# Loading the second block's x in steps between the columns of the first input projection

## The chip, the cores and the metric

The program runs on one core of one Trainium2 chip. The core has five engines that run their own queues of instructions: TensorE (PE: matmuls and transposes, which write PSUM; PEld is its loading of the fixed operand), VectorE (DVE), ScalarE (ACT), GpSimd (POOL, without access to PSUM) and SyncE (SP, which here asks for every DMA transfer). PSUM has eight banks of 512 float32 columns for 128 partitions. The metric is the device time of one execution in microseconds.

## The reference, cut to what matters

Two layers of a decoder trunk over 1040 tokens (16 meta tokens and 1024 of x) of width 1024. Each layer mixes the tokens and then applies an MLP:

```
h = concat(meta, x)
for layer in range(2):
    proj = rmsnorm(h) @ w_in[layer]          # 3336 columns, cut into the inputs of three mixers
    mixed = concat(hgrn2(...), gated_deltanet(...), s5(...))
    h = h + mixed @ w_out[layer]
    h = h + relu(rmsnorm(h) @ w1[layer])**2 @ w2[layer]
return rmsnorm(h)[:, 16:]
```

The gated DeltaNet's q, k and v (12 groups of 128 columns) pass through a causal convolution over four tokens and a SiLU; its gate z has four groups more. All is float32.

## The kernel before, in words

The 1040 tokens are two blocks of T = 520. Channels lie on partitions: a block's h is eight tiles of 128 x 520, of which there are eight buffers in all. Products are computed in three passes (high parts, low part of x, low part of w), 48 matmuls for a group of 128 columns ("a column" below), into a PSUM tile "pd" of two banks. There are two such tiles; every projection, the norm's scale and the loading of x take one in turn. Results pass through six SBUF tiles "s" of 128 x 520 on their way to DRAM.

`run` goes through block 0 and block 1 of the first layer, then the MLP of block 0, block 0 of the second layer (the third block of the program), and so on. `block` computes the norm, S5's two columns, the decay's rows, and then for each pair of heads four columns of q and k (`in_conv`, columns 0 to 7) and, window by window, the matrices of the DeltaNet (`gdn_decay`, which reads q and k back from DRAM). `gdn_solve` inverts their diagonal parts on VectorE and GpSimd, `s5_layer` prepares S5. Then come the columns 8 to 11 (v, again `in_conv`), four gates z (`in_gate`), and HGRN2's columns with its recurrence.

`early`, the generator that `block(0, 0)` gets as its `hook`, loads the second block's x. It takes the eight buffers of h after block 0's norm, calls `load_x(1, ...)` and then stores the second block's h to DRAM (`save_h`, eight transfers). `load_x` has ten parts, five windows of 104 tokens by two halves of 512 channels: a transfer into an "s" tile, four transposes on TensorE into one bank of a "pd" tile, four copies from there to h, by turns on ScalarE and VectorE. The block calls it whole, between `s5_layer` and column 8.

The order in the source is not the order of the queues: at build, a planner goes through the instructions with an estimate of their times and puts on each engine what is ready, the earlier in the source the sooner. The buffers of one name are given out in the order of the source. Two engines don't use one PSUM bank at the same time; the planner sets a wait between them. Weights are loaded ahead (`high_priority`).

Of the kernel before, what the change touches and what calls it, by code (L numbers as in the profile page):

```python
# [19 lines left out]
NMETA = 16  # L20
DEPTH = 2
T = 520
W = 104
# [7 lines left out]
NW = T // W  # L31
# [41 lines left out]
def pipeline(steps, gap):  # L73

    waiting, live, n = list(steps), [], 0
    while waiting or live:
        if waiting and n % gap == 0:
            live.append(waiting.pop(0))
        n += 1
        for g in list(live):  # L80
            if next(g, StopIteration) is StopIteration:
                live.remove(g)
        yield


def trace(*gens):

    live = list(gens)
    while live:
        for g in list(live):  # L90
            if next(g, StopIteration) is StopIteration:
                live.remove(g)


class Kern:
# [619 lines left out]
    def block(self, l, b, h, hook=None, first=False):  # L715

        xs = self.normed_rows(h, 8 * l, b)
        if first:
            self.save_h(b, h)
        self.Y = self.YS[b] = self.tl(self.dr, [KD, 128, T], "ydr", 2)  # L720
        if first:
            self.setup_mixers()
        g = {"z": self.tl(self.dr, [6, 128, T], "gated", 2)}
        us = self.in_s5(l, xs)
        g["rows"] = self.in_rows(l, b, xs)
        g["qkv"] = self.QKV = self.tl(self.dr, [12, 128, T], "qkvd", 2)
        self.gdn_begin(l, b, g)
        for p in range(2):
            for i in (2 * p, 2 * p + 1, 4 + 2 * p, 5 + 2 * p):
                self.in_conv(l, b, xs, i)  # L730
            trace(pipeline([self.gdn_decay(g, w, p) for w in range(NW)], GAP_DECAY))
        self.gdn_solve()
        self.gdn_scales()
        if b == 0:
            self.s5_layer(l)
        if hook:
            trace(hook)
        for i in range(8, 12):
            self.in_conv(l, b, xs, i)
        for i in range(4):  # L740
            self.in_gate(l, xs, C_GZ + 128 * i, g["z"][i])
        for j in range(2):
            hd = self.in_hgrn(l, xs, j)
            self.in_gate(l, xs, C_HG + 128 * j, g["z"][4 + j])
            trace(self.hgrn(l, b, j, hd, g["z"][4 + j]))
        self.grp = "t"
        trace(pipeline([self.gdn_state(l, g, w, p) for w in range(NW) for p in range(2)], GAP_STATE),
              self.lead(self.s5(l, b, us), AHEAD_S5))
        self.grp = "h"
# [499 lines left out]
    def load_x(self, b, h):  # L1249
        nc = self.nc  # L1250
        x = self.ins["x"][0]
        for w in range(NW):
            t0 = b * T + w * W - NMETA
            for k0 in (0, 4):
                xt = self.s()[:W, :512]
                cs = slice(128 * k0, 128 * k0 + 512)
                if t0 < 0:
                    nc.sync.dma_start(xt[0:NMETA, :], self.ins["meta"][:, cs])
                    nc.sync.dma_start(xt[NMETA:W, :], x[0:W - NMETA, cs])
                else:  # L1260
                    nc.sync.dma_start(xt, x[t0:t0 + W, cs])
                ps = self.tl(self.pd, [128, 2, 512], "pd", 2)[:, 0, :]
                for i in range(4):
                    nc.tensor.transpose(ps[:, i * W:(i + 1) * W], xt[:, i * 128:(i + 1) * 128], self.ident[:W, :W])
                for i in range(4):
                    copy = nc.vector.tensor_copy if i % 2 else nc.scalar.copy
                    copy(h[k0 + i][:, w * W:(w + 1) * W], ps[:, i * W:(i + 1) * W])
            yield

    def save_h(self, b, h):  # L1270
        self.H[b] = [self.spill(h[k], "hdr", 16) for k in range(KD)]
# [212 lines left out]
```

## Time and the profile before

| | us |
|---|---|
| median of three runs | 3055.49 |
| lowest and highest of the three | 3043.4 and 3062.02 |
| the profiled execution's own time | 3057.18 |
| its span, first to last instruction | 3055.4 |
| mean granted clock of TensorE in it, as a share of 2.4 GHz | 0.964 |

The profile is of one execution. Its times in rows are us from the first instruction; durations are us, or ns where that is said. A line such as L125 is the line of the kernel; helpers have one line for all their callers (L125 is every matmul, L113 every two-operand elementwise operation, L110 every activation), so the tiles' names tell them apart. In the views of waits, "A <- B" says that A stood still until B ended.

### The profile page before, as it was taken

What the parts mean: (1) busy time and instruction counts of PE and PEld (TensorE: products, weight loads), DVE (VectorE), ACT (ScalarE), POOL (GpSimd) and SP (SyncE); (2) the same over time, 40 slices, a digit from 0 to 9 for tenths busy, and PEclk for the clock granted to TensorE, in tenths of its full rate; (3) what the DMA queues carried; (4) which work ended last, traced back from release to release, by engine and by line L of the source; (5) the groups of instructions that cost most, each with busy time, mean ns of one, the idle gap of its engine ahead of it and who ended that gap; (6) DMA issues with size and microseconds to landing.
All of it is one profiled execution on the core that took longest, in us unless ns stands there. A gap on an engine that the chain in (4) does not pass through costs nothing.

```text
span 3055.4 us, 60525 instructions
## 1 busy us (share of the span) xinstructions
PE 2826.1 (92%) x23513; PEld 2637.9 (86%) x23513; DVE 1562.6 (51%) x2905; ACT 1298.7 (43%) x2657; POOL 1580.1 (52%) x1425
## 2 busy tenths in 40 slices
PE   7776899979999989878999998988999999999998
PEld 6775889978999989878999998986777788999998
DVE  7588664685532245787453224686554222522224
ACT  4434455534433345444444334543544333433332
POOL 4555465664644445747354444676464444444442
PEclk8898899989999999999999999999999999999999
DMA  5755555744433345555443334565443333533332
GB/s 148 193 125 160 141 154 138 213 95 125 126 96 96 91 141 142 161 142 149 130 115 96 94 91 142 144 152 152 113 125 98 100 96 95 163 91 90 93 91 80
DMA packets 641610, 381.17 MB, mean 125 GB/s; under 512 B 166239, under 2 KB 599237, under 8 KB 641325
## 3 DMA queue, kind: packets, MB, share of 16 engines
q1 hardware_dynamic: 641325, 377.31, 45.2%
q8 instruction: 186, 3.05, 0.4%
q14 instruction: 99, 0.81, 0.1%
HBM read 308.52 MB, written 70.43 MB: 124 GB/s over the span
## 4 chain that ended last, share of the span: by engine, by line
PE 45%; DVE 5%; issue 1%; DMA 1%; POOL 1%; ACT 1%; SPq 0%; DVEq 0%; POOLq 0%; ACTq 0%
PE pd L125 39%; PE mxt L125 4%; PE mxh L125 1%; DVE mh L113 1%; DVE s L116 1%; POOL wl L113 0%; DVE s L113 0%; ACT s L110 0%; DMA wr<-in_w_in_dram 0%; DVE s L121 0%; DMA nh<-rowd 0%; DVE mt L113 0%; POOL mh L113 0%; DVE ul L113 0%; DVE s L642 0%
## 5 line engine op out<-in xcount | busy, mean ns | idle before, releaser
L113 POOL TENSOR_TENSOR wl<-wr,wh 128x512 fp32r<-128x512 f32 x776 | 1025.2, 1323 | 1079.5 <-ACT wh L459 1012.3
L125 PE MATMUL pd<-xh,wh 128*128 128x260 f32 (+4 forms) x3688 | 832.3, 299 | 59.2 <-DVE s L116 21.2
L125 PE MATMUL pd<-xl,wh 128*128 128x260 f32 (+3 forms) x3688 | 830.1, 298 | 17.8 <-DVE xl L113 10.4
L459 ACT CAST wh<-wr 128x512 fp32r<-128x512 f32 x776 | 477.5, 617 | 862.5 <-PE pd L125 774.5
L125 PE MATMUL pd<-xh,wl 128*128 128x260 f32 (+2 forms) x3624 | 814.1, 299 | 11.0 <-POOL wl L113 10.7
L125 PEld LDWEIGHTS pd<-xh,wh 128*128 128x128 f32 (+1 forms) x3688 | 593.1, 192 | 81.4 <-issue 28.6
L125 PEld LDWEIGHTS pd<-xl,wh 128*128 128x128 f32 (+1 forms) x3688 | 594.4, 192 | 34.4 <-DVE xl L113 12.3
L125 PEld LDWEIGHTS pd<-xh,wl 128*128 128x128 f32 x3624 | 586.3, 193 | 27.2 <-POOL wl L113 13.5
L125 PE MATMUL pd<-uh,wh 128*128 128x260 f32 (+1 forms) x2008 | 469.5, 302 | 6.2 <-DVE h L113 3.6
L125 PE MATMUL pd<-ul,wh 128*128 128x260 f32 (+1 forms) x2008 | 470.5, 302 | 0.0
L125 PE MATMUL pd<-uh,wl 128*128 128x260 f32 (+1 forms) x2008 | 468.5, 302 | 1.2 <-POOL wl L113 1.2
L113 DVE TENSOR_TENSOR h<-h,pd 128x520 f32<-128x520 f32 (+2 forms) x296 | 200.4, 678 | 398.1 <-PE pd L125 395.5
L110 ACT ACTIVATE s<-s 128x520 f32<-128x520 f32 (+3 forms) x431 | 272.9, 635 | 196.5 <-DVE s L121 144.8
L125 PEld LDWEIGHTS pd<-uh,wh 128*128 128x128 f32 x2008 | 321.2, 189 | 22.3 <-issue 5.9
L125 PEld LDWEIGHTS pd<-uh,wl 128*128 128x128 f32 x2008 | 321.2, 189 | 15.4 <-POOL wl L113 2.1
L125 PEld LDWEIGHTS pd<-ul,wh 128*128 128x128 f32 x2008 | 321.4, 189 | 12.8
L116 DVE SCALAR_TENSOR_TENSOR s<-pd,r 128x520 f32<-128x520 f32 (+2 forms) x121 | 83.6, 692 | 330.8 <-PE pd L125 330.5
L113 DVE TENSOR_TENSOR ul<-s,uh 128x520 fp32r<-128x520 f32 (+1 forms) x129 | 97.7, 758 | 143.4 <-ACT uh L459 143.2
L113 POOL TENSOR_TENSOR s<-s 128x520 f32<-128x520 f32 x80 | 109.6, 1370 | 78.7 <-ACT s L110 67.9
L116 DVE SCALAR_TENSOR_TENSOR s<-pd,cvw,s 128x520 f32<-128x520 f32 x144 | 108.6, 754 | 46.4 <-ACT s L110 41.6
L113 POOL TENSOR_TENSOR mh<-mh,qh 128x260 f32<-128x260 f32 (+5 forms) x128 | 102.8, 827 | 29.9 <-ACT mh L110 29.3
L113 DVE TENSOR_TENSOR s<-s 128x520 f32<-128x520 f32 (+3 forms) x119 | 106.0, 895 | 21.8 <-ACT s L110 20.5
(255 smaller groups left out, 3187.9 us busy)
## 6 DMA issues: line engine op xcount, KB each, us to landing
wr<-in_mlp_w_dram SPq DMA_DIRECT2D x512, 256.0 KB
wr<-in_w_in_dram SPq DMA_DIRECT2D x208, 256.0 KB
wr<-in_w_out_dram SPq DMA_DIRECT2D x64, 256.0 KB
qkvd<-s SPq DMA_DIRECT2D x48, 260.0 KB
win<-qkvd SPq DMA_DIRECT2D x40, 312.0 KB
hdr<-h SPq DMA_DIRECT2D x32, 260.0 KB
mh<-qkvd SPq DMA_DIRECT2D x40, 208.0 KB
hd<-s SPq DMA_DIRECT2D x32, 260.0 KB
```

What stands on the lines that cost most here:

```text
L110: return self.nc.scalar.activation(out, in_, func, **kw)
L113: return (eng or self.nc.vector).tensor_tensor(out, a, b, op)
L116: return self.nc.vector.scalar_tensor_tensor(out, a, s, b, op0, op1)
L125: return self.nc.tensor.matmul(out, lhsT, rhs, start=start, stop=stop, **kw)
L459: self.nc.scalar.copy(hi, src)
```

## The change

`load_x` no longer yields once for a window of a block but, for the second block, once for each of the ten parts, and it asks for its transfers ahead: `ahead` is 0 for the first block and 1 for the second. A part's transposes come after the request for the next part. The block starts the generator where it called it before (that runs to the first request), and then takes two steps behind each of columns 8 to 11 and one behind each gate z; what is left is run behind the last gate. With ten parts, eight lie behind the columns, two behind the first two gates, and `save_h` behind the third. In both blocks a part's four transposes go to the two banks of the "pd" tile, two in each, where all four went to the first bank.

```diff
         if b == 0:
             self.s5_layer(l)
-        if hook:
-            trace(hook)
+        hook = hook or iter(())
+        next(hook, None)
         for i in range(8, 12):
             self.in_conv(l, b, xs, i)
+            next(hook, None)
+            next(hook, None)
         for i in range(4):
             self.in_gate(l, xs, C_GZ + 128 * i, g["z"][i])
+            next(hook, None)
+        trace(hook)
@@ load_x
-        for w in range(NW):
+        parts = [(w, k0) for w in range(NW) for k0 in (0, 4)]
+        got = {}
+
+        def get(w, k0):
             t0 = b * T + w * W - NMETA
...
+            cs = slice(128 * k0, 128 * k0 + 512)
+            got[w, k0] = xt = self.s()[:W, :512]
...
+                nc.sync.dma_start(xt, x[t0:t0 + W, cs])
+        ahead = b
+        for p in parts[:ahead]:
+            get(*p)
+        if ahead:
             yield
+        for n, (w, k0) in enumerate(parts):
+            if n + ahead < len(parts):
+                get(*parts[n + ahead])
+            xt = got.pop((w, k0))
+            ps = self.tl(self.pd, [128, 2, 512], "pd", 2)
+            for i in range(4):
+                nc.tensor.transpose(ps[:, i // 2, (i % 2) * W:(i % 2 + 1) * W], xt[:, i * 128:(i + 1) * 128], self.ident[:W, :W])
+            for i in range(4):
+                copy = nc.vector.tensor_copy if i % 2 else nc.scalar.copy
+                copy(h[k0 + i][:, w * W:(w + 1) * W], ps[:, i // 2, (i % 2) * W:(i % 2 + 1) * W])
+            if b:
+                yield
```

## Rows read from the trace of the kernel before

**Rows 1.** The page's first part: busy time, share of the span, instructions per engine.
```profile
PE 2826.1 (92%) x23513; PEld 2637.9 (86%) x23513; DVE 1562.6 (51%) x2905; ACT 1298.7 (43%) x2657; POOL 1580.1 (52%) x1425
```

**Rows 2.** Busy time by stretch (instructions in brackets), granted clock, DMA share, GB/s.
```profile
114.00:141.60 27.60, 13.11 (x73) 11.23 (x72) 15.05 (x45) 11.32 (x44) 10.27 (x12) 0.63 0.77 196
141.60:157.00 15.40, 15.34 (x115) 15.34 (x116) 8.32 (x19) 7.28 (x18) 8.39 (x9) 0.89 0.81 239
157.00:193.00 36.00, 23.74 (x174) 22.58 (x172) 35.23 (x54) 10.38 (x18) 23.31 (x15) 0.86 0.34 91
193.00:300.00 107.00, 76.13 (x588) 69.81 (x589) 90.67 (x209) 47.41 (x89) 58.47 (x51) 0.88 0.65 166
300.00:400.00 100.00, 84.11 (x917) 77.55 (x916) 69.07 (x139) 48.74 (x105) 46.41 (x50) 0.89 0.52 138
400.00:575.00 175.00, 173.23 (x1730) 162.91 (x1731) 91.24 (x195) 102.40 (x245) 112.99 (x114) 1.00 0.62 164
```

**Rows 3.** Waits in the stretch 114 to 157 us: total us, times, longest.
```profile
PE pd L1264 <- DMA s<-in_x_dram: 12.4, 5, 6.4
DVE h L1267 <- ACT h L1267: 10.2, 14, 2.5
```

**Rows 4.** Busy time of line 1264 (transposes) from 114 to 142 us.
```profile
114.00:142.00 28.00, 8.12 (x40) 6.32 (x40) 0.63 0.78 199
```

**Rows 5.** Timeline of TensorE, transposes of the first block.
```profile
13.68 0.58 PE L1264 MATMUL pd<-ident,s 104*128 104x104 f32 x4 [0.40 <-DVE h L1267]
...
15.47 0.58 PE L1264 MATMUL pd<-ident,s 104*128 104x104 f32 x4 [0.41 <-DVE h L1267]
```

**Rows 6.** Timeline of TensorE, matmuls of column 8.
```profile
142.27 0.64 PE L125 MATMUL pd<-xl,wh 128*128 128x264 f32 x2
...
145.41 0.41 PE L125 MATMUL pd<-xh,wh 128*128 128x264 f32 x2
```

**Rows 7.** Timelines of ScalarE and VectorE: column 8 emptied, gdn_solve's first step.
```profile
150.33 0.69 ACT L110 ACTIVATE s<-pd,cvw 128x520 f32<-128x520 f32 x1
...
151.05 2.35 DVE L116 SCALAR_TENSOR_TENSOR s<-pd,cvw,s 128x520 f32<-128x520 f32 x3 [0.25 <-ACT s L110]
153.44 0.43 DVE L121 TENSOR_SCALAR s<-s 128x520 f32<-128x520 f32 x1
157.02 1.10 DVE L121 TENSOR_SCALAR diag<-diag 80x676 f32<-80x676 f32 x1 [3.15 <-DMA diag<-MAd]
```

**Rows 8.** Timeline, SyncE's queue and TensorE: start, us, engine, line [idle before].
```profile
117.13 0.39 SPq L1261 DMA_DIRECT2D s<-in_x_dram  x1
...
120.50 0.93 PE L1264 MATMUL pd<-ident,s 104*128 104x104 f32 x4 [6.42 <-DMA s<-in_x_dram]
...
122.34 0.41 SPq L656 DMA_DIRECT2D qkvd<-s  x1
...
127.70 1.58 SPq L817 DMA_DIRECT2D mh<-qkvd  x3
...
159.31 0.34 SPq L656 DMA_DIRECT2D qkvd<-s  x1
```

**Rows 9.** Timelines, third block: SyncE's queue and VectorE.
```profile
1231.92 0.38 SPq L656 DMA_DIRECT2D qkvd<-s  x1
...
1237.43 0.45 SPq L656 DMA_DIRECT2D qkvd<-s  x1
...
1269.99 0.86 DVE L121 TENSOR_SCALAR diag<-diag 80x676 f32<-80x676 f32 x1 [3.69 <-DMA diag<-MAd]
```

**Rows 10.** Busy time of the instructions on tile h from 114 to 157 us.
```profile
114.00:157.00 43.00, 0.00 (x0) 0.00 (x0) 5.08 (x20) 4.61 (x20) 0.72 0.79 212
```

**Rows 11.** Busy time by stretch, third block, 1223.6 to 1270 us.
```profile
1223.60:1270.00 46.40, 44.10 (x367) 43.33 (x366) 30.24 (x54) 27.75 (x65) 35.58 (x33) 1.00 0.74 196
```

**Rows 12.** Busy time by stretch, clock beside TensorE's busy time.
```profile
13.00:17.00 4.00, 2.58 (x20) 1.60 (x17) 2.17 (x10) 2.28 (x10) 0.00 (x0) 1.00 0.43 135
117.50:131.50 14.00, 5.10 (x24) 3.90 (x24) 5.06 (x18) 5.50 (x19) 3.73 (x5) 0.50 0.84 220
```

More of the change, by code (lines that the diff above doesn't have):

```diff
@@ L1251, in load_x @@
         x = self.ins["x"][0]
-        for w in range(NW):
+        parts = [(w, k0) for w in range(NW) for k0 in (0, 4)]
+        got = {}
+        def get(w, k0):
             t0 = b * T + w * W - NMETA
[L1254 to L1267, printed above, removed]
-            yield
+            cs = slice(128 * k0, 128 * k0 + 512)
+            got[w, k0] = xt = self.s()[:W, :512]
+            if t0 < 0:
+                nc.sync.dma_start(xt[0:NMETA, :], self.ins["meta"][:, cs])
+                nc.sync.dma_start(xt[NMETA:W, :], x[0:W - NMETA, cs])
+            else:
+                nc.sync.dma_start(xt, x[t0:t0 + W, cs])
[3 more added lines that the diff above has]
+        if ahead:
+            yield
+        for n, (w, k0) in enumerate(parts):
[10 more added lines that the diff above has]
+                yield
     def save_h(self, b, h):
```

## The prediction

> **What bounds the kernel now.** The page's engine table comes first [rows 1]: TensorE is busy for 92% of the span, so over the whole program only what leaves TensorE idle, or running slowly, can be won. Next I cut the neighbourhood of the change into stretches [rows 2]. From 400 us on TensorE has 173.23 of 175 us; work that arrives there earlier makes the end earlier by as much. Before 400 us it isn't full, and the worst place is 114 to 141.6 us, just the stretch in which the second block's x is loaded: 13.11 of 27.60 us busy, at a mean granted clock of 0.63. The waits of that stretch [rows 3] name the reason: 12.4 us in five waits for x from DRAM. A transpose can't start before its transfer has landed, the transfers are asked for a few at a time, and the projections that follow need the two PSUM tiles "pd" and the six tiles "s" that the loading holds in turn.
>
> From 157 to 193 us another engine is full: VectorE has 35.23 of 36 us, TensorE 23.74 [rows 2]. That is gdn_solve, with the convolutions of columns 9 to 11 between its steps. So time won on TensorE before 157 us is worth something only if it takes work out of VectorE's way there.
>
> **Removed.** (a) The five waits, 12.4 us [rows 3]. (b) The clock: the forty transposes of this block take 8.12 us now [rows 4], while four in the first block, at the full clock, take 0.58 [rows 5]; ten such are 5.8, so 2.3 us less if they stand between projections that keep the clock up. (c) Column 8's first seven pairs of matmuls run at half clock, 0.64 us where later pairs take 0.41 [rows 6]: 7 x 0.23 = 1.6 us. Together 16.3 us of TensorE.
>
> **Added and moved.** The ten parts now stand one or two behind each column (8 behind columns 8 to 11, two behind the first gates). Their number, the copies and the transfers stay; only their place changes.
>
> PSUM: a part takes one of the two "pd" tiles, and a projection can no longer begin in the second tile while the first is emptied. Emptying a convolution takes 0.69 us on ScalarE and 2.35 on VectorE [rows 7], 3.0 in all; two parts' transposes fill 2 x 0.58 of it [rows 5]. Left is 1.9 us per column, four times 7.6 us. Behind a gate there is one part and one short operation empties the tile; I count nothing. The trace of before has no such order, so this is bounded: nothing, if the copies follow the transposes at once, and 4 x 3.0 = 12 us, if the copies wait on VectorE for the whole convolution. I take 7.6, since VectorE runs in order and the convolution comes first on it.
>
> The transfers: one that is asked for now lands some 3.4 us later (asked for at 117.13, its transposes at 120.50 [rows 8]). With one step ahead the odd parts have a column's matmuls in front of them, 24 pairs, and the others the wait for "pd" just counted. So their cover is the 1.9 us and the previous part's transposes; without it each even part would stand 2 to 3 us, which is inside the 12 us.
>
> SyncE's queue: each request waits for a free "s" tile, and weight loads, the decay's loads of q and k and the stores of the columns queue behind it. Now the loads of q and k go out at 127.70, though the last store they need went at 122.34, with requests for x between [rows 8]. The new order frees that, but it isn't worth 5 us: the third block of the program (second layer, first half of the sequence), the twin below, has the same stage without any x, and there gdn_solve begins 1269.99 - 1231.92 = 38.1 us behind that store, against 157.02 - 122.34 = 34.7 here [rows 7, 8, 9]. The chain of the decay sets this, and I leave it where it is. The eight stores of h move behind the second gate; their readers come much later. Nobody waits for h in the stretch, since the second block's norm stands behind all of the first block's projections. GpSimd gets none of the parts' instructions; ScalarE gets its twenty copies later, beside 10.38 of 36 us of work [rows 2], which hides them.
>
> VectorE: its twenty copies, 5.08 us [rows 10], lie in idle time now (it waits 10.2 us for ScalarE's copies of the same bank [rows 3]); some will fall behind 157 us. Against that, columns 9 to 11 leave the full stretch, 3 x (2.35 + 0.43) = 8.3 us [rows 7]. The twin confirms the size: from 8.3 us ahead of the same store to gdn_solve VectorE does 30.24 us [rows 11], here 15.05 + 8.32 less the copies, 18.3 [rows 2, 10]. So 12 us of work can go earlier, and at most 5 come back: 7 to 12 us.
>
> The first block's transposes are spread over the two banks of "pd". Now two engines empty one bank by turns, and each four transposes wait 0.40 us for it; two parts take 15.47 - 13.68 = 1.79 us [rows 5]. One link of four in the chain of copies falls away, some 0.2 us a part over the last five: 1 us, between 0 and 2, because squares stand between the copies on ScalarE.
>
> **The sum.** 16.3 - 7.6 = 8.7 on TensorE, inside VectorE's 7 to 12; with the start 9.7 us. The profiled execution took 3057.18 us with a span of 3055.4; 3057.2 - 9.7 = 3047.5. It lay 1.7 us above the median of the three runs, so the forecast on their scale is 3046 us.
>
> **Rivals.** (1) The whole stall goes. In the twin the next column is stored 1237.43 - 1231.92 = 5.5 us behind the last of the second pair, here 159.31 - 122.34 = 37.0 [rows 8, 9], so if "pd" costs nothing, 27.6 - 5.8 = 21.8 us go, with 1.6 for the clock and 2 at the start 25: 3030. For it speaks that TensorE in the twin has 44.10 of 46.40 us [rows 11]; against it VectorE, which is full behind either way.
>
> (2) The pair of PSUM tiles takes all of it back: 12 us of waits and all twenty copies behind 157 us (5.08): 16.3 - 17, no gain, 3056, and up to 3062, the slowest of the three runs. The Trainium skill (Perfetto Trace Analysis, "Optimizing Tensor Performance", Matmuls) says that independent matmul groups should rotate through PSUM banks so that emptying one overlaps the next group's matmuls; by that rule a transposing step between each two columns is what not to do, and this rival is its price. The trace agrees so far as VectorE's 2.35 us stand behind each column [rows 7], but it can't show the wait.
>
> (3) Slower: TensorE falls to half clock through columns 8 to 11 and the gates, because it now pauses behind each of them. In the first block the transposes kept 1.00 from 13 to 17 us with 2.58 of 4 us busy; from 117.5 to 131.5, with 5.10 of 14 busy, they stood at 0.50 [rows 12]. A column's 24 pairs cost 24 x 0.23 = 5.5 us more [rows 6], eight columns 44: 3046 + 44 = 3090. From the second such column on the gain is gone (9.7 / 5.5 = 1.8), and more than seven make it slower by 1%. Against it: through the twin's stretch, where TensorE pauses too, the clock stays at 1.00 [rows 11].
>
> (4) The change doesn't do what it says, because the instructions' order is planned at build: the parts bunch together where x was loaded before. Then only the first block's 1 us goes, 3054, inside "no change".
>
> **How the numbers follow.** Forecast (3038 to 3051) 0.5; rival 1 0.22; rival 2 and 4 together 0.23; rival 3 0.05. The three runs of before lie 18.6 us apart, so a median can sit some us off its case; the range has room for that. About 1% is what a measurement of this kernel can tell from no change: 30.5 us, so faster means below 3025 and slower above 3086. Rival 1's far side is 3020, ten us further, if the 7 to 12 us of VectorE come on top of TensorE's; the half of it below 3025 makes 0.12 for faster. Slower has 0.04, most of rival 3. The range runs from 3020 to rival 2's upper end, 3062.
>
> **What would show it.** Right: no wait of TensorE for x over 1 us between columns 7 and 8; column 8 stored some 6 to 10 us behind column 7 instead of 37; each of columns 8 to 11 followed by transposes and a wait of TensorE on VectorE of 1 to 3 us; the clock near 1.00 there; gdn_solve starting 34 to 40 us behind the store, with fewer convolutions inside. Wrong: waits for x that come back at the even parts, a gdn_solve that starts much earlier or later, or a stage that ends earlier while the stretch from 300 to 400 us, where TensorE has 84.11 of 100 [rows 2], gives the time back.

## Result: 0.8% slower, and the profile after

Five runs of the changed kernel have a median of 3078.09 us (3073.11 to 3082.23), against 3055.49 before: a ratio of 1.0079 with a 95% interval of 1.0052 to 1.0105. The forecast was 3046 us within 3020 to 3062, so the time lies outside the range, on the slow side. The profiled execution took 3078.23 us with a span of 3076.4, 21.0 us longer than that of before, at a mean granted clock of 0.954 (before 0.964).

The first part of the page, to set beside [rows 1]: the instructions are the same in number, and no engine has gained work worth the name.

```profile
PE 2841.9 (92%) x23513; PEld 2658.7 (86%) x23513; DVE 1561.4 (51%) x2905; ACT 1300.9 (42%) x2657; POOL 1575.1 (51%) x1425
```

TensorE's waits from 114 to 230 us, to set beside [rows 3]. The wait that the change was to take away has become three times as long:

```profile
PE pd L1279 <- DMA s<-in_x_dram: 37.9, 5, 15.7
PE mxh L417 <- DVE nh L121: 10.8, 2, 7.5
```

Busy time by stretch, cut as in [rows 2] and with the same columns (TensorE first, VectorE third, the granted clock behind GpSimd):

```profile
114.00:141.60 27.60, 15.55 (x117) 15.07 (x116) 13.50 (x30) 12.63 (x35) 12.64 (x13) 0.75 0.59 161
141.60:157.00 15.40, 6.66 (x47) 6.12 (x46) 11.49 (x26) 7.09 (x22) 10.32 (x12) 0.71 0.59 149
157.00:193.00 36.00, 18.59 (x111) 17.42 (x110) 29.27 (x65) 7.80 (x18) 15.82 (x9) 0.69 0.29 77
193.00:300.00 107.00, 83.12 (x662) 79.55 (x662) 79.01 (x197) 44.47 (x86) 55.36 (x47) 0.87 0.68 177
300.00:400.00 100.00, 86.79 (x888) 78.20 (x889) 73.09 (x146) 50.63 (x110) 45.79 (x52) 0.80 0.55 151
400.00:575.00 175.00, 167.29 (x1676) 157.11 (x1676) 102.55 (x199) 100.50 (x240) 110.98 (x113) 1.00 0.59 158
```

The first stretch is a little better than it was (15.55 us of TensorE against 13.11). The next two lose 8.68 and 5.15 us, and the full stretch of VectorE from 157 us is full no longer (29.27 against 35.23 of 36): nearly all of its idle time there is one wait for gdn_solve's first matrices, which come later than before.

```profile
DVE diag L121 <- DMA diag<-MAd: 5.3, 1, 5.3
```

From 193 to 400 us 9.7 us come back, as idle time of before is filled, and from 400 on 5.9 are lost again. By 575 us TensorE is 95 instructions behind before, counted from 114.

Where the waits stand is seen in TensorE's timeline; these are the transposes of the first eight parts (in brackets the idle time before them):

```profile
125.45 0.92 PE L1279 MATMUL pd<-ident,s 104*128 104x104 f32 x4 [5.24 <-DMA s<-in_x_dram]
133.19 0.93 PE L1279 MATMUL pd<-ident,s 104*128 104x104 f32 x4 [6.81 <-DMA s<-in_x_dram]
143.87 0.52 PE L1279 MATMUL pd<-ident,s 104*128 104x104 f32 x4
155.76 0.93 PE L1279 MATMUL pd<-ident,s 104*128 104x104 f32 x4 [4.56 <-DMA s<-in_x_dram]
164.80 0.52 PE L1279 MATMUL pd<-ident,s 104*128 104x104 f32 x4
170.92 0.93 PE L1279 MATMUL pd<-ident,s 104*128 104x104 f32 x4 [5.60 <-DMA s<-in_x_dram]
179.29 0.52 PE L1279 MATMUL pd<-ident,s 104*128 104x104 f32 x4
207.62 0.93 PE L1279 MATMUL pd<-ident,s 104*128 104x104 f32 x4 [15.65 <-DMA s<-in_x_dram]
```

And this is SyncE's queue over the same time: the requests for x (L1267) and the stores of the columns (L656).

```profile
120.99 0.39 SPq L1267 DMA_DIRECT2D s<-in_x_dram  x1
...
128.98 0.38 SPq L656 DMA_DIRECT2D qkvd<-s  x1
129.41 0.83 SPq L1267 DMA_DIRECT2D s<-in_x_dram  x2
133.47 0.45 SPq L656 DMA_DIRECT2D qkvd<-s  x1
152.66 0.81 SPq L1267 DMA_DIRECT2D s<-in_x_dram  x2
156.22 0.36 SPq L656 DMA_DIRECT2D qkvd<-s  x1
167.19 0.87 SPq L1267 DMA_DIRECT2D s<-in_x_dram  x2
...
196.02 2.71 SPq L913 DMA_DIRECT2D XD<-diag  x2
198.78 2.71 SPq L1267 DMA_DIRECT2D s<-in_x_dram  x2
```

The requests go out in twos. Behind the first, each even part (counted from one) is asked for in the same breath as the odd one after it, and its transposes come next on TensorE: 3.8 us after the request for the second part (129.41 to 133.19), 3.1 for the fourth, 3.7 for the sixth, 8.8 for the eighth. The odd part of the pair then has a column in front of it and waits for nothing. So three of the four transfers take what the prediction said, and the eighth part's takes longer for a reason that no run shows. They are asked for too late, and the next column stands behind the waiting transposes on TensorE. Column 8 is stored at 133.47, only 4.5 us behind column 7; the stores of columns 9, 10 and 11 follow at 156.22, 172.62 and 208.22.

Why just there? On ScalarE's timeline a column's first sigmoid, which writes its second tile "s", begins at 129.02, 152.64, 169.18 and 195.90:

```profile
129.02 1.97 ACT L110 ACTIVATE s<-s 128x520 f32<-128x520 f32 x3 [1.79 <-DVE s L121]
...
152.64 1.31 ACT L110 ACTIVATE s<-s 128x520 f32<-128x520 f32 x2
...
169.18 1.97 ACT L110 ACTIVATE s<-s 128x520 f32<-128x520 f32 x3 [1.88 <-DVE s L121]
...
195.90 1.97 ACT L110 ACTIVATE s<-s 128x520 f32<-128x520 f32 x3
```

A column takes two of the six tiles, one for the convolution and one for the sigmoid, and the tiles of one name are given out in the order of the source. A part asked for behind column 8 has its turn only when the second tile of column 8 has been given out. Three of the four pairs go out within 3 us behind that sigmoid, one 2 us ahead of it, so it is the plan's order rather than a signal that holds them. For the last pair the sigmoid itself is late: column 11 is first read on ScalarE at 179.81 us, and its sigmoid comes 16 us later, since VectorE has gdn_solve's and S5's steps before and between the operations of the convolution.

That is the theory which the experiments test: the request is late because it shares its tiles with the columns, and one step ahead is half a step for every second part.

### The profile page after: what moved, and what is told of

Same layout as the page of the kernel before. It is cut to its first block, busy times and chain, and to the rows that moved or that the text cites. A ratio compares the mean times of both kernels' runs of the same rounds, so it can differ in the third digit from the quotient of the medians.

```text
span 3076.4 us, 60536 instructions
## 1 busy us (share of the span) xinstructions
PE 2841.9 (92%) x23513; PEld 2658.7 (86%) x23513; DVE 1561.4 (51%) x2905; ACT 1300.9 (42%) x2657; POOL 1575.1 (51%) x1425
## 4 chain that ended last, share of the span: by engine, by line
PE 67%; DVE 10%; DMA 3%; issue 2%; ACT 1%; POOL 1%; SPq 0%; DVEq 0%; POOLq 0%; ACTq 0%
PE pd L125 57%; PE mxt L125 7%; DVE mh L113 3%; PE mxh L125 2%; DVE s L116 1%; DMA nh<-rowd 1%; DVE s L113 1%; DVE nh L113 1%; DMA wr<-in_w_in_dram 1%; ACT s L110 0%; DVE s L642 0%; DVE s L121 0%; DVE mt L113 0%; POOL wl L113 0%; DVE h L113 0%
## 5 line engine op out<-in xcount | busy, mean ns | idle before, releaser
L125 PEld LDWEIGHTS pd<-xh,wh 128*128 128x128 f32 (+1 forms) x3688 | 601.6, 195 | 81.8 <-issue 28.7
L125 PEld LDWEIGHTS pd<-xl,wh 128*128 128x128 f32 (+1 forms) x3688 | 601.8, 194 | 24.7 <-DVE xl L113 10.4
L125 PEld LDWEIGHTS pd<-xh,wl 128*128 128x128 f32 x3624 | 592.8, 195 | 20.8 <-POOL wl L113 6.5
L113 POOL TENSOR_TENSOR mh<-mh,qh 128x260 f32<-128x260 f32 (+5 forms) x128 | 99.2, 799 | 17.9 <-ACT mh L110 15.7
```

The source lines that it names most:

```text
L113: return (eng or self.nc.vector).tensor_tensor(out, a, b, op)
L125: return self.nc.tensor.matmul(out, lhsT, rhs, start=start, stop=stop, **kw)
```

## Experiments

Each ratio is against runs of the kernel before on the same chip, whose median was 3048.37 us for the first four, 3047.2 for the next four and 3046.09 for the last four. The changed kernel itself is not among these runs; its 0.8% is from the runs of the result. The ratios are those on record, and differ a little from the quotients of the medians. The times expected in the first four were set against a kernel before of 3055 us. Edits are shown against the changed kernel, cut to what matters. "Own tiles" are those of the name "ys", three buffers that the kernel has already for the mixers' results ahead of the output projection (`out_mlp`), a stage that comes later.

| | runs | median us | ratio | interval |
|---|---|---|---|---|
| one x for all ten parts | 10 | 3042.78 | 0.9977 | 0.9964 to 0.9991 |
| own tiles, three ahead | 10 | 3044.59 | 0.9985 | 0.9973 to 0.9998 |
| two banks alone | 10 | 3046.72 | 0.9989 | 0.9977 to 1.0002 |
| one step behind a column | 10 | 3053.71 | 1.0021 | 1.0005 to 1.0037 |
| own tiles, one ahead | 10 | 3044.86 | 0.9996 | 0.9982 to 1.0010 |
| tiles "s", three ahead | 10 | 3047.03 | 1.0003 | 0.9994 to 1.0013 |
| own tiles, three ahead, other PSUM | 7 | 3028.09 | 0.9946 | 0.9930 to 0.9962 |
| the same, called whole | 4 | 3029.22 | 0.9937 | 0.9914 to 0.9961 |
| other PSUM alone | 10 | 3042.30 | 0.9989 | 0.9978 to 1.0001 |
| x asked for by ScalarE | 6 | 3055.77 | 1.0032 | 1.0019 to 1.0046 |
| own tiles, three ahead, called whole | 10 | 3043.21 | 0.9987 | 0.9976 to 0.9998 |
| other PSUM, called whole | 10 | 3054.14 | 1.0021 | 1.0007 to 1.0035 |

**Is it x at all?** All ten parts are transposed from one tile, loaded once; nine transfers are left out, so the second block's h is not the reference's.

```diff
+            if b and got:
+                got[w, k0] = got["one"]
+                return
-            got[w, k0] = xt = self.s()[:W, :512]
+            got[w, k0] = xt = (self.tl(self.sp, [128, T], "ys", 3) if b else self.s())[:W, :512]
+            got["one"] = xt
```

> The second block's ten parts are all transposed from one tile, loaded once at the first step; nine of the ten transfers are left out, so that block's h is wrong. Places, transposes, PSUM tiles and copies stay as in the changed kernel. Theory (the odd parts wait for transfers that were asked for too late): no waits for x are left, about 3045 us, 10 below the kernel before. Rival (the pair of PSUM tiles): nothing changes there, 3070 to 3080 as in the changed kernel. Rival (banks or a new plan elsewhere): also 3070 or more.

(Its "odd parts" are counted from zero; they are the even parts above.) The slowdown is gone, and TensorE's largest wait from 114 to 230 us is another one, for the copies that empty a part's tile:

```profile
PE pd L1283 <- DVE h L1286: 16.9, 4, 6.5
```

The one x also lies in a tile of another name, so this run takes away the transfers and the shared tile together. It shows that x, as it is brought, makes the change slow, and behind it stands a price of the PSUM pair that is twice what was predicted.

**Bringing x earlier, from tiles of its own.**

```diff
-            got[w, k0] = xt = self.s()[:W, :512]
+            got[w, k0] = xt = (self.tl(self.sp, [128, T], "ys", 3) if b else self.s())[:W, :512]
-        ahead = b
+        ahead = 3 * b
```

> The changed kernel with the second block's x in three tiles of its own (buffers of the MLP that are unused here, "ys") and asked for three steps ahead. Theory (late requests): each part has a column in front of it, waits for x fall from 37.9 us to under 5, time 3040 to 3050. Rival (PSUM pair): transposes still wait for VectorE, 3070 or more. Rival (plan elsewhere): 3065 or more.

All transfers are made, and the waits for x are gone as in the kernel with one x. What is left is the wait for the copies, 20.1 us; it is the view of waits, then VectorE and TensorE around the longest:

```profile
PE pd L1279 <- DVE h L1282: 20.1, 4, 8.8
```

```profile
162.92 0.52 PE L1279 MATMUL pd<-ident,ys 104*128 104x104 f32 x4
...
164.02 0.24 ACT L1282 COPY h<-pd 128x104 f32<-128x104 f32 x1
...
168.99 0.59 DVE L113 TENSOR_TENSOR mh<-Tm,diag 80x242 f32<-80x242 f32 x1
169.51 0.74 DVE L116 SCALAR_TENSOR_TENSOR s<-pd,cvw,s 128x520 f32<-128x520 f32 x1
...
170.49 0.25 DVE L1282 COPY h<-pd 128x104 f32<-128x104 f32 x1
...
172.25 0.95 PE L1279 MATMUL pd<-ident,ys 104*128 104x104 f32 x4 [8.81 <-DVE h L1282]
```

The part's first copy is made on ScalarE at 164.02; the second stands in VectorE's queue behind gdn_solve's steps and an operation of the convolution until 170.49. A short copy pays for whatever the plan put ahead of it.

**The two banks alone**, in the kernel before; nothing else of the change is made.

```diff
-                ps = self.tl(self.pd, [128, 2, 512], "pd", 2)[:, 0, :]
+                ps = self.tl(self.pd, [128, 2, 512], "pd", 2)
-                    nc.tensor.transpose(ps[:, i * W:(i + 1) * W], ...)
+                    nc.tensor.transpose(ps[:, i // 2, (i % 2) * W:(i % 2 + 1) * W], ...)
...
```

> The kernel before with one part of the change alone: a part's four transposes go to two banks of the PSUM tile. Theory (late requests): within 5 us of the kernel before, 3050 to 3060. Rival (banks or a new plan): a good part of the 22 us, 3065 or more.

The interval holds no change and the 1 us that was predicted alike. This part costs nothing that can be seen.

**One step behind a column.** Then every part has a column in front of it.

```diff
             self.in_conv(l, b, xs, i)
             next(hook, None)
-            next(hook, None)
```

> The changed kernel with one step behind each of columns 8 to 11 in place of two (one behind each gate as before, the last two parts behind the last gate). Theory (late requests): every part but the last has a column between its request and its transposes, so the 5 to 15 us waits shrink to 1 or 2 us, 3045 to 3058. Rival (PSUM pair): one part behind each column costs nearly as much as two, 3065 or more.

One wait for x is left, 4.0 us, but the time is only part of the way back: TensorE now waits 8.2 us for the copies in front of columns, 5.3 behind gdn_solve and 8.6 for the convolutions. Two steps in a row are thus not the whole of it.

**Own tiles with one step ahead, and three ahead with the shared tiles.** This is the pair that parts the tile from the distance.

```diff
-            got[w, k0] = xt = self.s()[:W, :512]
+            got[w, k0] = xt = (self.tl(self.sp, [128, T], "ys", 3) if b else self.s())[:W, :512]
```

> The changed kernel with the second block's x in three tiles of its own, still asked for one step ahead. Theory (distance: of two steps in a row the second has only its predecessor's four transposes between its request and its own): waits for x stay at 15 to 30 us, 3060 to 3075. Rival (the tiles "s", shared with the columns, hold the requests back): waits under 10 us, 3045 to 3050.

```diff
-        ahead = b
+        ahead = 3 * b
```

> The changed kernel, its x in the shared tiles "s" as there, asked for three steps ahead. Distance theory: waits for x under 8 us, 3043 to 3052. Rival (tiles): four of six tiles are held by x, columns and requests wait for each other, 3060 or more.

Each theory missed in one of the two: with own tiles the distance theory's waits didn't come, and with the shared tiles three ahead the tile theory's loss didn't. Either remedy is enough. With own tiles and the same single step, the requests go out singly at 122.02, 127.39, 137.43 and 143.47 us, no wait for x is left, and the copies take its place:

```profile
PE pd L1279 <- DVE h L1282: 17.4, 4, 7.0
```

With the shared tiles three ahead, the second and third parts get their tiles ahead of column 8's, and are asked for at 119.86 and 122.50 instead of 129.41; one wait for x of 4.4 us is left beside 11.4 us for copies. Both times are those of before. The loss of the change is undone by one word at the tile, without moving a transpose in the source.

**x asked for from ScalarE's queue**, to take SyncE's order out.

```diff
-                nc.sync.dma_start(xt, x[t0:t0 + W, cs])
+                (nc.scalar if b else nc.sync).dma_start(xt, x[t0:t0 + W, cs])
```

> The changed kernel with the second block's x asked for from ScalarE's queue and not SyncE's. If the requests stand in SyncE's order behind stores and gdn_solve's writes: waits for x fall under 12 us, 3042 to 3055. If they are late because their tile "s" is handed out late: 25 us or more of waits, 3068 to 3085.

The waits for x remain, and the requests still come together. On ScalarE's timeline they now stand right behind the column's sigmoid:

```profile
129.07 0.64 ACT L110 ACTIVATE s<-s 128x520 f32<-128x520 f32 x1 [1.78 <-DVE s L121]
129.15 0.83 ACTq L1267 DMA_DIRECT2D s<-in_x_dram  x2
...
168.95 0.64 ACT L110 ACTIVATE s<-s 128x520 f32<-128x520 f32 x1 [2.26 <-DVE s L121]
169.01 0.74 ACTq L1267 DMA_DIRECT2D s<-in_x_dram  x2
```

```profile
PE pd L1279 <- DMA s<-in_x_dram: 35.2, 5, 9.7
```

So the queue isn't what makes them late: in either queue the plan puts them behind the sigmoid, where the shared tile has its turn. The last wait is longer on SyncE's queue (15.7 us where this kernel has 9.7): there the eighth part's request stands behind gdn_solve's results (XD, 196.02) and goes out at 198.78, here at 195.30; the rest is a longer time from request to transposes (8.8 us against 6.5), which no run explains. The time missed what was expected for waits of this size, 3068 to 3085 us. With almost the same waits this kernel is 0.3% slower than before, where the change, in the runs of the result, was 0.8% slower.

**The PSUM price taken away too.** The second block's parts go to "mxt", the PSUM tiles of the decay's transposes, instead of "pd".

```diff
-            ps = self.tl(self.pd, [128, 2, 512], "pd", 2)
+            if b:
+                pt = self.mps("t")
+                at = [pt[:, i * W:(i + 1) * W] for i in range(4)]
...
-                nc.tensor.transpose(ps[:, i // 2, (i % 2) * W:(i % 2 + 1) * W], ...)
+                nc.tensor.transpose(at[i], ...)
...
```

With own tiles and three ahead as well:

> Own tiles for x, three steps ahead, and the second block's transposes go to the PSUM tiles of the decay ("mxt", idle there) and not to the pair "pd" of the columns. If the pair costs time on the path that sets the end: the 20.1 us in which transposes waited for copies go, 3025 to 3038. If VectorE hides it: no change against the run without this step, 3040 to 3048.

With this edit alone:

> The changed kernel with the second block's transposes in "mxt" instead of "pd"; x in "s", one step ahead, as there. If late requests alone make the loss: waits for x stay above 20 us, 3060 to 3078. If the PSUM pair is what lets them fall behind: 3040 to 3050.

The second of these came out against the theory of late requests. With "mxt" alone x is still in the shared tiles and still one step ahead, and its first pair is asked for at 128.26 us, hardly earlier than the 129.41 of the changed kernel; yet no wait for x is left from 114 to 230 us, and the loss is gone. Its timelines of SyncE and TensorE (matmuls 264 wide are those of columns 8 to 11, 260 wide those of the gates):

```profile
128.26 0.89 SPq L1267 DMA_DIRECT2D s<-in_x_dram  x2
...
143.03 0.41 PE L125 MATMUL pd<-xh,wl 128*128 128x264 f32 x2
...
144.74 0.52 PE L1284 MATMUL mxt<-ident,s 104*128 104x104 f32 x4
...
146.03 0.47 PE L125 MATMUL pd<-xh,wh 128*128 128x260 f32 x2 [0.76 <-DVE s L116]
```

All four columns are computed before the first part's transposes, so the transfers have landed by then and no column stands behind a part. In these runs a late request thus makes a stall only where the part also keeps its place in front of the next column, as it does while both take "pd" in turn.

Both remedies together gain 0.54% [0.38, 0.70], some 16 us; own tiles and three ahead without "mxt" gave 0.15%, "mxt" without them 0.11%, with an interval that just holds no change. Busy time by stretch of the kernel with both:

```profile
114.00:157.00 43.00, 39.68 (x336) 39.06 (x334) 32.20 (x60) 26.67 (x69) 34.49 (x33) 1.00 0.73 196
157.00:200.00 43.00, 29.71 (x225) 29.08 (x225) 36.58 (x66) 14.57 (x35) 26.44 (x17) 0.90 0.57 169
```

From 114 to 157 us TensorE now has 39.68 us of work where it had 28.45 before [rows 2], at the full clock, and column 11 is stored at 155.06, ahead of gdn_solve's start (166.85). Here too the columns 8 to 11 come first; the parts stand among the gates, three of them from 149.68 to 155 and seven from 158.83 to 177 us. The tiles "mxt" were not idle, as the expectation has it: the decay's products use them too, the last eight from 148.94, and the first part follows 0.7 us behind that.

**Was the place in the source needed?** The kernels of this group call the generator whole again, between `s5_layer` and column 8, as before.

```diff
-        hook = hook or iter(())
-        next(hook, None)
+        if hook:
+            trace(hook)
         for i in range(8, 12):
             self.in_conv(l, b, xs, i)
-            next(hook, None)
-            next(hook, None)
         for i in range(4):
             self.in_gate(l, xs, C_GZ + 128 * i, g["z"][i])
-            next(hook, None)
-        trace(hook)
```

With own tiles, three ahead and "mxt":

> The kernel before in its order (x loaded whole, between the S5 preparation and column 8), but x in own tiles asked for three parts ahead and transposes in "mxt", so that the planner may put columns between the parts. If shared buffers, not the place in the source, cause the stall of before: its 12.4 us of waits go, 3025 to 3040. If the place causes it: 3045 to 3056.

With own tiles and three ahead, in "pd":

> The order of the kernel before (x loaded whole) with x in own tiles, three parts ahead, transposes still in "pd". If the tiles "s" make the stall of before: 3025 to 3038. If the pair "pd" does: 3040 to 3050, the columns still standing behind the last part.

With "mxt", shared tiles and nothing ahead:

> The order of the kernel before with transposes in "mxt", x still in the tiles "s" without asking ahead. If "pd" makes the stall of before: 3025 to 3038. If the tiles "s" do: 3042 to 3052.

Not needed. With both resources free the kernel that calls the loading whole gains as much, 0.63% [0.39, 0.86] in four runs. Its source has x ahead of column 8, but on TensorE the columns 8 to 11 come first and the parts stand among the gates, as in the kernel that steps:

```profile
141.92 0.41 PE L125 MATMUL pd<-xh,wl 128*128 128x264 f32 x2
...
149.39 0.52 PE L1280 MATMUL mxt<-ident,ys 104*128 104x104 f32 x4
149.69 0.48 PE L125 MATMUL pd<-xh,wh 128*128 128x260 f32 x2
...
151.70 0.52 PE L1280 MATMUL mxt<-ident,ys 104*128 104x104 f32 x4
```

So the order that gains is not x between the columns, which the change was after, but x behind them. With one of the two free the kernel gains 0.1% (own tiles) or is 0.2% slower ("mxt", 3054.14 us where 3042 to 3052 stood for the tiles "s"; there the first waits are 12.4 us for the decay's loads and 10.3 for the convolutions). In each of these x stays ahead of columns: with own tiles in "pd" all ten parts lie ahead of column 8 (110.85 to 132 us, the column from 133.92), with "mxt" and the tiles "s" nine lie ahead of column 9 (145.21 to 155, the column from 157.41).

## Why the prediction was wrong, step by step

**The step that failed is "The transfers".** It saw that every second part would have no column in front of it, and priced that at "2 to 3 us ... inside the 12 us". The measured waits of the even parts are 6.81, 4.56, 5.60 and 15.65 us, with 5.24 for the first part 37.9 in all, more than the 12.4 that were to go. The landing time was right (3.4 us estimated, 3.1 to 3.8 measured for three of four); the time of the request was taken from the source. There it stands in front of another part's transposes. In the queue it goes out behind the column's second tile, since it takes one of the same six, and the two steps in a row leave nothing between it and its transposes. The text had noted "each request waits for a free 's' tile", but only as a nuisance for what queues behind the request, not as the date of the request itself. That the tile sets the date is shown by own tiles alone (no wait for x, time of before), by the shared tiles given out earlier (one wait of 4.4 us), and by the other queue (waits stay). The late date makes the loss only together with "pd": with the transposes in "mxt", and the first pair asked for 1.2 us earlier, no wait for x is left and the time is that of before. The text had the pair "pd" as a price beside the transfers (rival 2), not as what holds each part in front of the next column. That it does so by the order in which its tiles are given out fits these runs and was not tested by itself, since each kernel's order is planned anew. The Trainium skill (Perfetto Trace Analysis, "Identifying Performance Opportunities", Optimization Strategy) says that a gap which repeats on the engine that should be full can mean that there isn't enough SBUF or PSUM for the next tile. The four gaps of 4.56 to 15.65 us agree, and three tiles that the columns don't use close them. The six tiles alone, asked for three ahead, close them as well, but for one wait of 4.4 us; so here it is the order in which the tiles are given out more than their number.

**The PSUM pair** was right as a mechanism in the main (it is a part's transposes that wait, where the text had the projection) and too small as a term: 7.6 us, at most 12, against 16.9 to 20.1 us in four waits in the three kernels in which x doesn't come first. The bound of 12 counted the convolution as all that can stand in front of a copy; the timeline shows gdn_solve's steps there as well. In the changed kernel itself this wait doesn't appear, because the waits for x lie over it. Rival 2 named the Trainium skill's rule (Perfetto Trace Analysis, "Optimizing Tensor Performance", Matmuls) on rotating through PSUM banks. These runs agree: own tiles and three ahead gain 0.15% in "pd" and 0.54% in "mxt". The step to "mxt" takes away the waits for copies and also puts the columns ahead of x, and the two effects aren't told apart.

**The rest of the removed.** The transposes take 7.24 us from 114 to 224 us where 8.12 was to become 5.8 [rows 4]: half of them still stand behind a wait and run slower (0.92 where the others take 0.52). Column 9's matmuls begin at 0.64 us a pair, as column 8's did [rows 6].

**What held.** gdn_solve starts 163.64 - 128.98 = 34.7 us behind the last store it needs, as in [rows 7, 8]; it starts 6.6 us later in all, since that store does. The two banks cost nothing. The parts do stand between the columns in the changed kernel, so rival 4 is out. Rival 3's lower clock is there (0.69 to 0.75 from 114 to 193 us, on the mean between the levels of 1.2 and 2.4 GHz), but column 9's slow pairs come right behind a wait of 6.81 us. In the kernel with own tiles and "mxt", whose ten parts stand among the gates, the granted clock is 1.00 from 114 to 157 us and 0.93 from 157 to 193. So parts among projections don't bring the clock down by themselves, and the clock here is more likely the waits' effect than their cause; that is argued, not shown. With one x for all parts, and so without waits for x, the time is some 7 us under that of before, near the 9.7 of the sum; as the PSUM wait is twice its term there, that is in part luck. The text also named the sign that came, "waits for x that come back at the even parts"; the failure was to give it no price and no rival of its own.

**What stays open.** Counted to 1231 us, TensorE has done 617 + 3496 + 5540 = 9653 instructions against 622 + 3591 + 5614 = 9827; 174 of them at the mean of 2841.9 / 23513 = 0.121 us are an estimated 21 us, the whole difference. But 74 of these fall behind 575 us, far from the change (busy time by stretch, after and then before):

```profile
114.00:575.00 461.00, 378.00 (x3496) 353.48 (x3494) 308.91 (x658) 223.13 (x510) 250.91 (x244) 0.88 0.58 154
575.00:1231.00 656.00, 615.65 (x5540) 594.59 (x5539) 319.03 (x551) 268.83 (x549) 339.26 (x316) 0.96 0.43 116
```

```profile
114.00:575.00 461.00, 385.67 (x3591) 359.42 (x3591) 309.60 (x657) 227.53 (x517) 259.84 (x249) 0.91 0.60 158
575.00:1231.00 656.00, 618.08 (x5614) 596.12 (x5613) 332.40 (x582) 275.30 (x574) 350.18 (x327) 0.97 0.44 119
```

The kernel that asks from ScalarE has done 3603 instructions from 114 to 575 us in spite of 35.2 us of the same waits, a few more than before. So a loss of this size can be made good in the idle time from 200 to 400 us, and why the change didn't make it good, the shorter eighth wait apart, no run settles. The whole order is planned anew for each kernel, and what a microsecond of this stage is worth differs: four waits of 17 to 20 us in all cost nothing against before, while the two stepped kernels without them gained 0.5% and 0.1%. The kernel with "mxt" alone, at 0.1%, has the columns ahead of x as the one with both, at 0.5%; no run says what separates the two.

## What to carry to other kernels

Before transposes or loads are spread between compute groups, list every buffer that the two share, in the order in which it is given out: a prefetch that takes its tile from the compute's own pool is asked for when the compute lets it, not when the source asks. Free all of the shared resources at once, here SBUF tiles and PSUM: in the stepped order either one alone took back the loss of 0.8% and gained 0.15% at most, and the two together gained 0.5 to 0.6%. With a planner that orders by readiness they also let it choose the order: it put the columns first and x among the gates behind them. Moving the calls in the source was neither needed nor enough.

## What the hardware showed that was not expected

Emptying a PSUM tile of transposes, four copies of 0.25 us, held TensorE for up to 8.81 us, because two of the four stood in VectorE's queue behind gdn_solve's steps and a convolution. And a stall can be worth much less than its length: the kernel that asks from ScalarE has 35.2 us of waits for x against 12.4 in the kernel before, and is 0.32% [0.19, 0.46] slower, about 10 us.
